# Small matrix products issued in pieces of 32, three steps moved from VectorE to ScalarE, and an earlier split of two head pairs, in a hybrid decoder trunk on one Trainium2 core

## The chip, the cores and the metric

One core of a Trainium2 chip runs the whole kernel. Its engines are TensorE (PE: matrix products; its weight loads are listed as PEld), VectorE (DVE), ScalarE (ACT), GpSimd (POOL) and SyncE (SP), which here issues DMAs. The metric is the device time of one execution in microseconds (us); less is better.

## The reference

One mixer layer over 16 meta tokens and 512 tokens, model width 2048, float32. One input projection feeds three causal mixers that work on different heads; their outputs are gated, joined, projected back and added to the input, and a last RMSNorm follows.

```python
proj = (rms_norm(x, norm_w) @ w_in)                 # 2048 -> about 7600 columns
# A) gated DeltaNet, 6 heads x 128, chunks, triangular solve, state carried from chunk to chunk
# B) GLA, 5 heads (dk 64, dv 128), chunks of 64:
log_g = log_sigmoid(gl @ w_gk2 + b_gk) / 16.0       # gate, bias added before it
g = cumsum(log_g)                                   # within a chunk
attn = einsum('bhid,bhjd,bhijd->bhij', q, k, exp(g_i - g_j))   # causal
k_dec = k * exp(g_last - g);  s = s * exp(g_last) + k_dec^T v
# C) forgetting attention, 5 heads x 128, blocks of 128 queries:
probs = softmax(q @ k^T + c_i - c_j)                # causal, c = cumsum(log f)
o = concat(norm(A) * silu(z), norm(B) * silu(z), C * silu(z))
return rms_norm(x + o @ w_out)[:, 16:]
```

## The kernel before

All large products are made in two float32r halves: an operand `w` is split into `hi` (a rounded copy, made by ScalarE) and `lo` (the rest, made by VectorE), and a product is three matmuls, `hi*hi`, `hi*lo`, `lo*hi`, each of 128x512 (or 128x264 in the pairs below). The stages follow one another on PE like this:

- `pz`, `pg`, `pbdz`, `pbgz`: first gate columns and small gates.
- `px`: the pairs of input columns (DeltaNet's q, k, v; GLA's and attention's k and v), each pair by a scheme of seven half-size products.
- fill blocks `pbgq`, `pbfq`, `pbgz`, `pbfz`: the remaining input columns (queries and gate paths of GLA and attention), 16 groups of three 128x512 matmuls each. They depend on nothing but their operands, so they are what PE does while the mixers wait.
- DeltaNet (`pm`, `pn`, `pym`, `pks`, `p`, `po`), in the order of time between about 512 and 580 us.
- GLA (`gla_load`, `gla_pair`, `gla_levels`, `gla_out`) and attention (`fox_load`, `fox_head`, `fox_block`, `fox_out`), from about 580 to 823 us, side by side.
- the output projection: `po` (three of eight pairs of heads, kp 0 to 2, plus kp 5), `ps` (`SEV`: the four pairs kp 3, 4, 6, 7, again by seven products), and `pz` (the last column block).

**GLA's levels.** `gla_levels` makes the causal 128x128 gate-weighted scores of a pair of heads from small products: for a block size of 64 and 32 together 24 products, then for (16, 8), (4, 2) and (1, 0) 64 products of 32x32 each (half as many for the last, single head). They go to the banks `pss`, one bank for each head. `kx` and `qx` are the scaled keys and queries of a level, `gd` their decay, `at` and `a32` the score tiles. A float32 product that is not a transpose stands as two matmul records and two weight loads in the profile. In `gla_pair`, `gkd` is the block decay times keys, `pkd` the bank of its transposes and of the state products, `gst` the states; `pgo` is the output bank, `gon` its normalised copy. In `gla_load`, `pgk` is the bank of the gate product, `gu` its biased copy.

**Attention's blocks.** `fox_block` makes the logits of 128 queries (`pfa`, `pfd`), takes the maximum (VectorE, `fsm`), the exponential and its sum (ScalarE, `fp`), the reciprocal of the sum (VectorE), multiplies by it, transposes the result on PE into `pfa` and splits it (`ph` by ScalarE, `pl` by VectorE). `fox_out` transposes the meta tokens' part into the bank `pfw`, splits it in four turns between ScalarE (`mh`) and VectorE (`ml`), and then makes the products with the values (`pfw`). `pvf` and `pvgv` are the banks in which attention's and GLA's values (`fv`, `vgv`) are transposed.

**What sets the order.** The program is recorded by a planner, `Weave`: each step is a generator that yields instructions, slots to wait for or events. `Weave.run` always emits the list of instructions with the least planned start plus a priority, and each engine then executes in exactly the order of emission (`pin`). A list that a generator yields is emitted whole. PE's instructions are of two kinds, light (`op.light`: fewer than 64 columns, or fewer than 128 rows or columns of the weights) and heavy; the planner stays in one kind for a turn:

```python
ran = t - self.since
if self.mode:
    other = ran + (sum(o.dur for o in c[3]) if c[3][0].light else 0.0) > LIGHT
else:
    other = ran >= HEAVY
```

A DMA is planned no earlier than the planned end of all DMA traffic less `BACK[...]` (the first number up to a planned time of `BT` on PE, the second after it). Nearly all DMAs are issued by SP in the order of emission; an issue that waits holds back the ones behind it.

**Head pairs.** `finish` hands the gated output of a head over. For the pairs in `STK = (3, 4, 6, 7)`, `seven_heads(kp)` splits both heads and their sums (`oh`/`ol`, `os`, `sh`/`sl`) and sets `e_head`. It starts after `e_d`, which waits for all heads of GLA and attention, or, for a pair in `EARLY_KP`, after GLA and head 10. `seven_operands` splits the weights of `ps` (`wh`, `wl`) once the pairs are there. All instructions carry the line of the planner's call (L283).

Of the kernel before, what the change touches and what calls it, by code (L numbers as in the profile page):

```python
# [8 lines left out]
F32 = mybir.dt.float32  # L9
# [4 lines left out]
AF = mybir.ActivationFunctionType  # L14
ALU = mybir.AluOpType
# [3 lines left out]
P = 128  # L19
D = 2048  # L20
KT = D // P
NM = 16
S = 512
T = NM + S
HT = T // 2
NB = S // P
EPS = 1e-6
H = 3
NN = NB * H
# [52 lines left out]
STP, IP = 0.0, 0.05  # L82
GP, KX = (), 5
AP, KA, XP, GAP = -0.2, 2, 0.3, 0.1
BACK, BT = (3.0, 1.5), 100.0
LIGHT, SLACK, DMAL, STL = 2.0, 0.25, 1.1, 2.5
HEAVY, NEAR = 1.5, 0.05
KW = 2
NXP, SQP, NSL = -0.6, 0.0, 1.5
LP, LSL = 0.1, 1.0  # L90
WP, AOP, HDP = 1.0, -0.6, 0.0
EARLY_KP = ()
STK, KOS, OS0, OSN, OSP = (3, 4, 6, 7), 3, 1, 2, 0.1


# [265 lines left out]
def tile_hybrid_trunk(ctx, tc, xT, xtok, mtok, w_gate, w_first, w_in, w_out, consts, lmask, fin_w, out):  # L361
# [169 lines left out]
    zs, spill = {}, {}  # L531
# [1 line left out]
    e_sp, e_bank = {}, {}  # L533
    sp_of = lambda key: e_sp.setdefault(key, Ev())

    def silu_row(z, key, dst):
        if key[0] == "dz" or key in EARLY:
            yield A.activation(z, z, AF.Silu)
            yield SP.dma_start(out=dst, in_=z)
            return  # L540
        t = yield Get(row_s, f"st{key[0]}{key[1]}")
        yield V.tensor_scalar_max(t[:, :S], z, LOW)
        yield A.activation(t[:, :S], t[:, :S], AF.Exp, scale=-1.0)
        yield A.activation(t[:, :S], t[:, :S], AF.Ln, bias=1.0)
        yield A.activation(t[:, :S], t[:, :S], AF.Exp, scale=-1.0)
        yield VT(out=z, in0=z, in1=t[:, :S], op=ALU.mult)
        row_s.give(t)
        yield SP.dma_start(out=dst, in_=z)
# [174 lines left out]
    def token_rows(key, c, u):  # L723
# [29 lines left out]
    other_pairs = [(("gk", 0), ("gk", 1)), (("gv", 0), ("gv", 1)), (("gv", 2), ("gv", 3)), (("gv", 4), ("gk", 2))] \  # L753
        + [(("fk", h), ("fv", h)) for h in range(FOX_HEADS)]
    PAIRS = [p for c in zip(conv_pairs, other_pairs) for p in c]
    xpart = lambda k0, s: tuple((lambda j, t=t: t[k0 + j][:, s]) for t in (xh, xl))
    tpart = lambda d, s: tuple((lambda j, w=w: d[j // 2][w][:, j % 2, s]) for w in range(2))
    RHS = {1: xpart(0, L), 2: xpart(8, L), 3: xpart(8, R), 4: tpart(tb_, L), 5: tpart(ta, L), 6: tpart(tb_, R),
# [79 lines left out]
    def store(p, n, u):  # L838
        yield VT(out=u, in0=u, in1=rstd, op=ALU.mult)
        key = p.keys[n]  # L840
        if key[0] in CONV:
            c = yield Get(row_s, f"cv{p.i}{n}")
            yield from conv(u, key, c, u)
            if key[0] != "dv":
                yield spilled(key, c)
            W.go(token_rows(key, c, u), -0.1, f"rows{key[0]}{key[1]}", 3.0)
        else:
            yield spilled(key, u)
            sp_of(key).set()
# [252 lines left out]
    def levels(g):  # L1102
        s = gs[g]
        an, xc, xm, um = s.an, s.xc, s.xm, s.um
        uc = yield Get(m_s, f"uc{g}", (P, NN, 32))
        yield V.transpose(uc.rearrange("p n c -> p (n c)"), xc.rearrange("p n c -> p (n c)"))
        pm = yield Get(bank_s, f"pm{g}")
        p3 = pm[:, : NN * 32].rearrange("p (n c) -> p n c", c=32)
        lh = [(slice(64 * q, 64 * q + 32), slice(64 * q + 32, 64 * q + 64)) for q in range(2)]
        yield [PE.matmul(p3[lo_, n, :], an[hi_, n, lo_], uc[hi_, n, :], start=True, stop=True)  # L1110
               for n in range(NN) for lo_, hi_ in lh]
        m1 = yield Get(m_s, f"m1{g}", (P, NN, 32))
        for q in range(2):
            yield A.copy(m1[64 * q : 64 * q + 32], p3[64 * q : 64 * q + 32])
        W.go(state0(g), 0.0, f"state{g}")
        yield V.transpose(um.rearrange("p h c -> p (h c)"), xm.rearrange("p h c -> p (h c)"))
        e_um[g].set()
        yield [PE.matmul(p3[a, n, :], l[lo_, n, :], r[lo_, n, :], start=True, stop=True)
               for n in range(NN) for lo_, hi_ in lh for a, l, r in ((lo_, xc, m1), (hi_, m1, xc))]
        l1 = yield Get(m_s, f"l1{g}", (P, NN, 32))  # L1120
        yield A.copy(l1, p3)
        bank_s.give(pm)
        m_s.give(m1)
        s.uf = uf = yield Get(big_s, f"uf{g}", (P, NN, P))
        yield G.memset(uf, 0.0)
        for r in range(4):
            c = slice(32 * r, 32 * r + 32)
            yield A.copy(uf[c, :, c], uc[c])
        m_s.give(uc)
        for q in range(2):  # L1130
            yield V.tensor_copy(uf[64 * q : 64 * q + 32, :, 64 * q + 32 : 64 * q + 64], l1[64 * q : 64 * q + 32])
# [167 lines left out]
    SC = 1.0 / 16.0  # L1299
# [26 lines left out]
    def gla_load(p, ev):  # L1326
        ne = 2 if p < 2 else 1
        kT, qT, gc = yield from many(Get(w_s, f"g{n}{p}", keep=4) for n in ("kT", "qT", "gc"))
        if p < 2:
            yield from fetch(("gk", p), kT)  # L1330
            yield sp_of(("gq", p))
            yield SP.dma_start(out=qT[:, NM:], in_=spill["gq", p])
        else:
            for t in (kT, qT):
                yield G.memset(t[64:], 0.0)
            yield from fetch(("gk", p), kT[:64], slice(0, 64))
            yield from fetch(("gk", p), qT[:64], slice(64, P))
            yield V.tensor_scalar_mul(qT[:64], qT[:64], 0.125)
        vt = yield from many(Get(w_s, f"vt{p}{e}", keep=4) for e in range(ne))
        vm = yield Get(t_s, f"vm{p}")  # L1340
        yield G.memset(vm, 0.0)
        ev2 = evs(*range(ne))
        for e in range(ne):
            W.go(tok_values(("gv", 2 * p + e), vt[e], vm, e, ev2[e]), GPRI + 0.1, f"gv{p}{e}")
        u = (yield Get(w_s, f"gu{p}", keep=1))
        t = (yield Get(w_s, f"gt{p}", keep=1))
        pg = yield from many(Get(bank_s, f"pgk{p}{a}", keep=1) for a in range(2))
        yield [PE.matmul(pg[a][:, :HT], wgk[:, P * p : P * p + P], misc[:, a * HT : (a + 1) * HT], start=True, stop=True)
               for a in range(2)]
        for a in range(2):  # L1350
            yield V.tensor_scalar_add(u[:, a * HT : (a + 1) * HT], pg[a][:, :HT], bgk[:, p : p + 1])
            bank_s.give(pg[a])
        yield V.scalar_tensor_tensor(out=t, in0=u, scalar=-1.0, in1=u, op0=ALU.mult, op1=ALU.min)
        yield A.activation(t, t, AF.Exp)
        yield A.activation(t, t, AF.Ln, bias=1.0)
        yield V.scalar_tensor_tensor(out=u, in0=u, scalar=0.0, in1=t, op0=ALU.min, op1=ALU.subtract)
        yield V.tensor_tensor_scan(gc, gsc, u, 0.0, ALU.mult, ALU.add)
        w_s.give(u)
        w_s.give(t)
        yield tuple(ev2.values())  # L1360
        ev.set((ne, kT, qT, gc, vt, vm))
# [3 lines left out]
    def gla_levels(p, group, sets, pair, at, a32, ev):  # L1365
# [8 lines left out]
        for s in group:  # L1374
# [10 lines left out]
                        mm.append(PE.matmul(pss[e][o0 : o0 + n, off + b * n : off + b * n + n], kx[rr, k0 : k0 + n],  # L1385
                                            qx[rr, q0 : q0 + n], start=True, stop=True))
            off += NB * n
        yield mm
        for s in group:
            if ops[s][0]:  # L1390
                sets.append(ops[s][0])
# [48 lines left out]
    def gla_pair(p, pair, sets, at):  # L1440
# [6 lines left out]
            W.go(gla_levels(p, g, sets, pair, at, a32, el[g]), GPRI, f"levs{p}{g[0]}")  # L1447
        dd = yield Get(w_s, f"gkd{p}")
        d4 = dd[:, :S].rearrange("p (b t) -> p b t", b=NB)
        yield VT(out=d4, in0=g4[:, :, P - 1 : P].to_broadcast([P, NB, P]), in1=g4, op=ALU.subtract)  # L1450
        yield A.activation(dd[:, :S], dd[:, :S], AF.Exp, scale=SC)
        yield VT(out=d4, in0=d4, in1=k4, op=ALU.mult)
        pk = yield Get(bank_s, f"pkd{p}")
        yield [PE.transpose(pk[:, b * P : (b + 1) * P], dd[:, b * P : (b + 1) * P], ident) for b in range(NB)]
# [83 lines left out]
    ST = STK  # L1538
# [82 lines left out]
    def fox_block(h, b, ld, phi, plo, mt, ev):  # L1621
# [22 lines left out]
        yield A.activation(pr[:, : m + P], pr[:, : m + P], AF.Exp, bias=sm[:, 2:3], accum_out=sm[:, 3:4])  # L1644
        yield V.reciprocal(sm[:, 0:1], sm[:, 3:4])
        yield V.tensor_scalar_mul(m4[:, b, :NM], pr[:, :NM], sm[:, 0:1])
        yield V.tensor_scalar_mul(pr[:, NM : m + P], pr[:, NM : m + P], sm[:, 0:1])
        yield [PE.transpose(pa[:, jb * P : (jb + 1) * P], pr[:, NM + jb * P : NM + (jb + 1) * P], ident)
               for jb in range(b + 1)]
        n = min(b + 1, 3)  # L1650
# [163 lines left out]
                    s.src[kp, n].set(t)  # L1814

    def seven_operands():
        yield tuple(e_head[2 * kp] for kp in ST)
        for s in SEV:
            for n in ORDER:
                for kp in ST:  # L1820
                    src = yield s.src[kp, n]
                    hi = yield Get(d_s, f"wh{s.cp}{kp}{n}", (P, S), F32R)
                    lo = yield Get(d_s, f"wl{s.cp}{kp}{n}", (P, S), F32R)
                    yield A.copy(hi, src)
                    yield VT(out=lo, in0=src, in1=hi.bitcast(F32), op=ALU.subtract)
                    give(src, r_s, d_s)
                    s.op[n, kp].set((hi, lo))
# [271 lines left out]
```

## Time and profile before

| what | value |
|---|---|
| runs shown (device time) | 970.83, 973.27, 974.09 us; median 973.27 |
| the profiled execution: its own time, its span | 971.76 us, 970.0 us |
| granted TensorE clock over the span | 0.995 |
| busy: PE, PEld, DVE, ACT, POOL | 947.7, 844.5, 750.5, 569.6, 67.1 us |
| DMA | 167.18 MB, mean 172 GB/s |
| chain that ended last, by engine | PE 90%, DVE 3%, ACT 3%, issue 1%, DMA 1% |

The span runs from the first to the last instruction; 1.8 us of the execution's own time lie around it. A busy time is the union of an engine's instructions; PE's matmuls overlap in the pipeline, so that a busy PE can still be losing time, and what counts is how far apart they start (0.23 us for 128x512, 0.12 us for 128x264). "Idle before" is the time in which an engine ran nothing before an instruction, and the name behind the arrow is what ended it; "issue" means that no wait in the profile explains it.

### The profile page before, as it was taken

Reading aid. Unit: us, or ns where it says so; the run is one execution under the profiler, and the core shown is the slowest. Engines: PE = TensorE matmul, PEld = TensorE weight load, DVE = VectorE, ACT = ScalarE, POOL = GpSimd, SP = SyncE. Lnnn points to the kernel's source line nnn. Section 1 sums busy time; section 2 is a strip of 40 time slices with the busy share of each in tenths; the row PEclk is TensorE's granted clock in tenths of the full one; section 3 lists DMA queues with packets and bytes.
Section 4 is the critical chain, followed back from the end, with each engine's and each line's share of the span. In section 5 each row is a group of like instructions: output and inputs, shape, how many; then the busy total and the mean of one; then the engine's idle time right before and its main releaser. Section 6 shows DMA issues by size and latency. Waiting matters only on the chain.

```text
span 970.0 us, 19077 instructions
## 1 busy us (share of the span) xinstructions
PE 947.7 (98%) x7283; PEld 844.5 (87%) x7283; DVE 750.5 (77%) x1337; ACT 569.6 (59%) x1205; POOL 67.1 (7%) x118
## 2 busy tenths in 40 slices
PE   9999999999999999999999999989989999999996
PEld 7888999999999999999987997778777787888885
DVE  7986887888888888798973666876866966888775
ACT  7865566667766576654424684637546565345445
POOL 0000101010100101110001111010010100000000
PEclk9999999999999999999999999999999999999999
DMA  9933648658784768692288335423233365474424
GB/s 344 372 113 132 164 136 226 191 150 228 193 228 117 220 154 253 171 229 83 89 290 292 97 88 182 141 85 137 99 100 135 107 207 182 154 261 153 151 67 173
DMA packets 92143, 167.18 MB, mean 172 GB/s; under 512 B 16253, under 2 KB 36477, under 8 KB 92052
## 3 DMA queue, kind: packets, MB, share of 16 engines
q1 hardware_dynamic: 87156, 157.31, 49.2%
q0 software_dynamic: 4608, 8.39, 6.5%
q8 instruction: 57, 0.93, 0.4%
q14 instruction: 34, 0.28, 0.1%
q10 hardware_dynamic: 288, 0.27, 0.1%
HBM read 142.33 MB, written 40.39 MB: 188 GB/s over the span
## 4 chain that ended last, share of the span: by engine, by line
PE 90%; DVE 3%; ACT 3%; issue 1%; DMA 1%; POOL 0%; SPq 0%; DVEq 0%; ACTq 0%; POOLq 0%
PE px L283 38%; PE po L283 9%; PE ps L283 8%; PE pz L283 5%; PE pbfq L283 5%; PE pbfz L283 5%; PE pbgz L283 4%; PE pbdz L283 2%; PE pbgq L283 2%; PE pg L283 1%; PE pss L283 1%; PE pfa L283 1%; PE pks L283 1%; PE pfw L283 1%; PE pgo L283 1%
## 5 line engine op out<-in xcount | busy, mean ns | idle before, releaser
L283 DVE SCALAR_TENSOR_TENSOR lp<-a,hp 128x1024 fp32r<-128x1024 f32 x90 | 110.7, 1231 | 36.9 <-ACT hp L283 36.1
L283 ACT CAST hp<-a 128x1024 fp32r<-128x1024 f32 x90 | 94.5, 1050 | 73.3 <-PE px L283 48.0
L283 PE MATMUL px<-xh,hp 128*128 128x264 f32 x432 | 123.7, 286 | 0.0
L283 PE MATMUL px<-xh,lp 128*128 128x264 f32 x432 | 122.7, 284 | 0.0
L283 PE MATMUL px<-xl,hp 128*128 128x264 f32 x432 | 122.7, 284 | 0.0
L283 PE MATMUL px<-tah,hp 128*128 128x264 f32 x288 | 83.8, 291 | 0.0
L283 PE MATMUL px<-tbh,hp 128*128 128x264 f32 x288 | 82.5, 287 | 0.0
L283 PE MATMUL px<-tbh,lp 128*128 128x264 f32 x288 | 82.3, 286 | 0.0
L283 PE MATMUL px<-tbl,hp 128*128 128x264 f32 x288 | 82.0, 285 | 0.0
L283 PE MATMUL px<-tah,lp 128*128 128x264 f32 x288 | 82.0, 285 | 0.0
L283 PE MATMUL px<-tal,hp 128*128 128x264 f32 x288 | 81.8, 284 | 0.0
L283 PEld LDWEIGHTS px<-xh,hp 128*128 128x128 f32 x432 | 81.4, 188 | 0.1
L283 PEld LDWEIGHTS px<-xh,lp 128*128 128x128 f32 x432 | 81.3, 188 | 0.0
L283 PEld LDWEIGHTS px<-xl,hp 128*128 128x128 f32 x432 | 81.2, 188 | 0.0
L283 PEld LDWEIGHTS px<-tbh,hp 128*128 128x128 f32 x288 | 54.3, 189 | 0.1
L283 PEld LDWEIGHTS px<-tah,hp 128*128 128x128 f32 x288 | 54.2, 188 | 0.1
L283 ACT CAST hp<-s 128x1024 fp32r<-128x1024 f32 x36 | 37.8, 1051 | 28.0 <-PE px L283 19.2
L283 PEld LDWEIGHTS px<-tal,hp 128*128 128x128 f32 x288 | 54.3, 188 | 0.0
L283 PEld LDWEIGHTS px<-tbl,hp 128*128 128x128 f32 x288 | 54.2, 188 | 0.0
L283 PEld LDWEIGHTS px<-tah,lp 128*128 128x128 f32 x288 | 54.2, 188 | 0.0
L283 PEld LDWEIGHTS px<-tbh,lp 128*128 128x128 f32 x288 | 54.2, 188 | 0.0
L283 DVE SCALAR_TENSOR_TENSOR lp<-s,hp 128x1024 fp32r<-128x1024 f32 x36 | 44.0, 1221 | 7.9 <-ACT hp L283 7.9
(406 smaller groups left out, 2642.2 us busy)
## 6 DMA issues: line engine op xcount, KB each, us to landing
a<-in_w_in SPq DMA_DIRECT2D x72, 512.0 KB, 5.7
osum<-in_w_out SPq DMA_DIRECT2D x32, 256.0 KB, 5.0
o<-in_w_out SPq DMA_DIRECT2D x16, 512.0 KB, 3.5
kd<-osum SPq DMA_DIRECT2D x25, 256.0 KB, 3.8
kd<-in_w_out SPq DMA_DIRECT2D x21, 256.0 KB, 4.2
rgz<-in_w_in SPq DMA_DIRECT2D x10, 512.0 KB
rfq<-in_w_in SPq DMA_DIRECT2D x10, 512.0 KB, 3.2
rfz<-in_w_in SPq DMA_DIRECT2D x10, 512.0 KB, 3.2
```

The lines of the kernel that those rows point to most:

```text
L283: self.pin(op.call(*op.a, **op.kw))
```

## The change

```diff
-BACK, BT = (3.0, 1.5), 100.0
-LIGHT, SLACK, DMAL, STL = 2.0, 0.25, 1.1, 2.5
+BACK, BT = (3.0, 3.0), 100.0
+LIGHT, SLACK, DMAL, STL = 1.5, 0.25, 1.1, 2.5
+NOP, CH, CD = 0, 32, 32
-EARLY_KP = ()
+EARLY_KP = (3, 4)
 # levels (DeltaNet), at two places
-        yield [PE.matmul(...) for n in range(NN) for lo_, hi_ in lh]
+        mm = [PE.matmul(...) for n in range(NN) for lo_, hi_ in lh]
+        for i in range(0, len(mm), CD):
+            yield mm[i : i + CD]
 # gla_load
-            yield V.tensor_scalar_add(u[:, a * HT : (a + 1) * HT], pg[a][:, :HT], bgk[:, p : p + 1])
+            yield A.activation(u[:, a * HT : (a + 1) * HT], pg[a][:, :HT], AF.Identity, bias=bgk[:, p : p + 1])
 # gla_levels
-        yield mm
+        for i in range(0, len(mm), CH):
+            yield mm[i : i + CH]
 # gla_pair
-        yield VT(out=d4, in0=g4[:, :, P - 1 : P].to_broadcast([P, NB, P]), in1=g4, op=ALU.subtract)
-        yield A.activation(dd[:, :S], dd[:, :S], AF.Exp, scale=SC)
+        gl = one((P, NB), f"ggl{p}")
+        yield A.activation(gl, g4[:, :, P - 1], AF.Copy, scale=SC)
+        for b in range(NB):
+            yield A.activation(d4[:, b], g4[:, b], AF.Exp, scale=-SC, bias=gl[:, b : b + 1])
 # fox_block
-        yield V.tensor_scalar_mul(pr[:, NM : m + P], pr[:, NM : m + P], sm[:, 0:1])
+        yield A.activation(pr[:, NM : m + P], pr[:, NM : m + P], AF.Copy, scale=sm[:, 0:1])
 # seven_operands
-        yield tuple(e_head[2 * kp] for kp in ST)
+        yield e_d
         for s in SEV:
             for n in ORDER:
+                if n == ORDER[NOP]:
+                    yield tuple(e_head[2 * kp] for kp in ST)
...
```

The lists of small products are yielded 32 at a time, and a light turn of the planner is at most 1.5 of its microseconds long (2.0 before). The scaling of the probabilities by the reciprocal sum, the addition of GLA's gate bias and the block decay are ScalarE's; the decay is four exponentials of 128x128 with a bias in place of one subtraction and one exponential of 128x512. After a planned time of 100 us DMAs may be planned 3.0 instead of 1.5 us ahead of the end of the traffic. The pairs 3 and 4 may be split after GLA. The rest of the diff (a gate path in `store`, `EXTRA`) is reached by no pair of columns. The numbers of instructions on DVE and ACT go from 1339 to 1310 and from 1064 to 1102; those on PE, POOL and SP stay.

Since each list now competes separately, the whole order behind the first pieces differs. Three places:

PE, GLA's first pair of heads. Before, the end of the list for the levels 4 and 2 (`pss_7521`, `pss_7522`), attention's first logits, and the start of the next list (levels 1 and 0):

```order
L283 MATMUL pss_7521<-qx_6892,kx_6877 32x32
L283 MATMUL pss_7522<-qx_6892,kx_6877 32x32
L283 MATMUL pfa_7538<-fk_7012,fq_7014 128x144
L283 MATMUL pfa_7539<-fk_7012,fq_7014 128x272
L283 MATMUL pfa_7540<-fk_7012,fq_7014 128x400
L283 MATMUL pss_7630<-qx_6892,gkT_6917 32x32
L283 MATMUL pss_7631<-qx_6892,gkT_6917 32x32
```

Now, within the list for the levels 4 and 2 (`pss_7559`, `pss_7560`), the end of its first piece and the start of its second:

```order
L285 MATMUL pss_7559<-qx_6901,kx_6894 32x32
L285 MATMUL pss_7560<-qx_6901,kx_6894 32x32
L285 MATMUL pbfz_7532<-xh_255,hbfz_0_7309 128x512
L285 MATMUL pbfz_7532<-xl_256,hbfz_0_7309 128x512
L285 MATMUL pbfz_7532<-xh_255,lbfz_0_7310 128x512
L285 MATMUL pfa_7454<-ident,fp_7461 128x128
L285 MATMUL pbfz_7532<-xh_269,hbfz_0_7309 128x512
L285 MATMUL pbfz_7532<-xl_270,hbfz_0_7309 128x512
L285 MATMUL pbfz_7532<-xh_269,lbfz_0_7310 128x512
L285 MATMUL pss_7559<-qx_6882,kx_6874 32x32
L285 MATMUL pss_7560<-qx_6882,kx_6874 32x32
```

What was one run of 64 products is two, with fill products and a transpose of attention between them.

SP, the start of GLA and attention behind DeltaNet: loads of attention's first keys (`fk`), queries (`fq`), values (`fv`) and gates (`fcb`), a store of queries (`spfq`), and a load of fill weights (`rgz`). Before:

```order
L283 DMA rgz_6814<-in_w_in 128x1024
L283 DMA fk_6878<-spfk_3549 128x528
L283 DMA spfq_6890<-qfq_6887 128x512
L283 DMA fq_6879<-spfq_5878 128x512
L283 DMA rgz_6900<-in_w_in 128x1024
L283 DMA fv_6880<-spfv_3736 128x528
L283 DMA fcb_6930<-gd 128x528
```

Now:

```order
L285 DMA fk_6875<-spfk_3549 128x528
L285 DMA fq_6876<-spfq_5881 128x512
L285 DMA fv_6877<-spfv_3736 128x528
L285 DMA fcb_6898<-gd 128x528
L285 DMA spfq_6896<-qfq_6890 128x512
L285 DMA gkT_6917<-spgk_1472 128x528
L285 DMA rgz_6910<-in_w_in 128x1024
```

A store of queries (`spfq`) stood ahead of the loads of `fq`, `fv` and `fcb`, and a load of fill weights ahead of `fv`; now both stand behind all four loads.

DVE before, at the last block of attention's first head (`fp_7047`: its probabilities):

```order
L283 RECIPROCAL fsm_7048<-fsm_7048 128x1
L283 TENSOR_SCALAR fmt_7020<-fp_7047,fsm_7048 128x16
L283 TENSOR_SCALAR fp_7047<-fp_7047,fsm_7048 128x512
L283 TENSOR_TENSOR pl_7018<-pfa_7024,ph_7013 128x128
L283 SCALAR_TENSOR_TENSOR gd_7132<-ggc_6919 128x8x32
```

ACT now, around the scaling of the same block (`fp_7028`):

```order
L285 ACTIVATE fp_7021<-fp_7021,fsm_7022 128x384
L285 ACTIVATE fp_7028,fsm_7029<-fp_7028,fsm_7029 128x528
L285 CAST ph_6996<-pfa_7009 128x128
L285 ACTIVATE fp_7028<-fp_7028,fsm_7029 128x512
L285 CAST ph_6998<-pfa_7009 128x128
L285 CAST hbfq_0_7149<-rfq_6982 128x1024
```

The scaling stood right behind the reciprocal on DVE; now it stands on ACT, behind the exponential, with one cast between the two.

More of the change, by code (lines that the diff above doesn't have):

```diff
@@ L90 @@
 LP, LSL = 0.1, 1.0
+EXTRA = ()
+NOP, CH, CD = 0, 32, 32
 WP, AOP, HDP = 1.0, -0.6, 0.0
-EARLY_KP = ()
+EARLY_KP = (3, 4)
 STK, KOS, OS0, OSN, OSP = (3, 4, 6, 7), 3, 1, 2, 0.1
@@ L534, in tile_hybrid_trunk, with silu_row @@
     sp_of = lambda key: e_sp.setdefault(key, Ev())
-    def silu_row(z, key, dst):
-        if key[0] == "dz" or key in EARLY:
+    def silu_row(z, key, dst, early=False):
+        if early or key[0] == "dz" or key in EARLY:
             yield A.activation(z, z, AF.Silu)
@@ L755, in tile_hybrid_trunk @@
     PAIRS = [p for c in zip(conv_pairs, other_pairs) for p in c]
+    for i, p in EXTRA:
+        PAIRS.insert(i, p)
     xpart = lambda k0, s: tuple((lambda j, t=t: t[k0 + j][:, s]) for t in (xh, xl))
@@ L840, in store @@
         key = p.keys[n]
-        if key[0] in CONV:
+        if key[0] in ("gz", "fz"):
+            spill[key] = drp.tile([P, S], F32, name=f"sp{key[0]}{key[1]}")
+            yield from silu_row(u[:, NM:], key, spill[key], True)
+            sp_of(key).set()
+        elif key[0] in CONV:
             c = yield Get(row_s, f"cv{p.i}{n}")
@@ L1109, in levels @@
         lh = [(slice(64 * q, 64 * q + 32), slice(64 * q + 32, 64 * q + 64)) for q in range(2)]
-        yield [PE.matmul(p3[lo_, n, :], an[hi_, n, lo_], uc[hi_, n, :], start=True, stop=True)
-               for n in range(NN) for lo_, hi_ in lh]
+        mm = [PE.matmul(p3[lo_, n, :], an[hi_, n, lo_], uc[hi_, n, :], start=True, stop=True)
+              for n in range(NN) for lo_, hi_ in lh]
+        for i in range(0, len(mm), CD):
+            yield mm[i : i + CD]
         m1 = yield Get(m_s, f"m1{g}", (P, NN, 32))
@@ L1117, in levels @@
         e_um[g].set()
-        yield [PE.matmul(p3[a, n, :], l[lo_, n, :], r[lo_, n, :], start=True, stop=True)
-               for n in range(NN) for lo_, hi_ in lh for a, l, r in ((lo_, xc, m1), (hi_, m1, xc))]
+        mm = [PE.matmul(p3[a, n, :], l[lo_, n, :], r[lo_, n, :], start=True, stop=True)
+              for n in range(NN) for lo_, hi_ in lh for a, l, r in ((lo_, xc, m1), (hi_, m1, xc))]
+        for i in range(0, len(mm), CD):
+            yield mm[i : i + CD]
         l1 = yield Get(m_s, f"l1{g}", (P, NN, 32))
```

## The prediction

> **What bounds the kernel now.** I read first the page's busy times and its chain, then the busy times by stage, then what PE waited for between 500 and 825 us.
>
> ```profile
> PE 947.7 (98%) x7283; PEld 844.5 (87%) x7283; DVE 750.5 (77%) x1337; ACT 569.6 (59%) x1205; POOL 67.1 (7%) x118
> ...
> q8 instruction: 57, 0.93, 0.4%
> ...
> PE 90%; DVE 3%; ACT 3%; issue 1%; DMA 1%; POOL 0%; SPq 0%; DVEq 0%; ACTq 0%; POOLq 0%
> ```
>
> PE carries the chain from end to end. The change neither adds nor removes a product, so the time can only move by what PE loses: pauses, a lower clock, and turns between small and large products. The stages (us; busy by engine, with the number of instructions; then granted clock, DMA share, GB/s):
>
> ```profile
> 575.00:825.00 250.00, 238.12 (x2182) 191.24 (x2180) 178.58 (x481) 143.38 (x386) 18.01 (x36) 0.99 0.41 137
> 825.00:970.00 145.00, 137.06 (x604) 111.41 (x602) 108.54 (x181) 68.94 (x131) 0.00 (x0) 0.99 0.48 159
> ```
>
> GLA and attention (575 to 825) leave PE idle for 11.9 us and also keep DVE busy for 179 of 250; from 825 on PE idles only in the 8 us behind its last product. So the place is 500 to 825, and there PE waited for (total, times, longest):
>
> ```profile
> PE pss L283 <- issue: 5.1, 3, 2.6
> PE pfw L283 <- DVE ml L283: 2.0, 3, 1.3
> PE pkd L283 <- DVE gst L283: 1.9, 2, 1.1
> PE pvf L283 <- DMA fv<-spfv: 0.7, 1, 0.7
> PE pm L283 <- DVE uc L283: 0.7, 1, 0.7
> PE pvgv L283 <- DMA vgv<-spgv: 0.7, 1, 0.7
> PE pgo L283 <- ACT gon L283: 0.6, 1, 0.6
> ```
>
> With four smaller ones (0.2 to 0.4 each, 1.2 together) these are 12.9 us; 5.1 of them end for no semaphore, inside GLA's small products. That group first.
>
> **The pauses in the small products.** Stretches around two of the three:
>
> ```profile
> 640.00:644.00 4.00, 3.56 (x209) 2.71 (x193) 2.61 (x14) 0.51 (x2) 0.00 (x0) 1.00 0.91 330
> 646.20:650.00 3.80, 3.76 (x44) 2.84 (x45) 2.64 (x14) 1.80 (x7) 0.00 (x0) 0.55 0.01 2
> 713.20:720.72 7.52, 6.01 (x127) 4.75 (x128) 4.08 (x11) 2.88 (x7) 0.00 (x0) 1.00 0.46 143
> 716.00:720.00 4.00, 3.24 (x107) 2.46 (x106) 1.60 (x4) 1.72 (x5) 0.00 (x0) 1.00 0.50 158
> 720.00:725.00 5.00, 4.27 (x45) 3.40 (x45) 1.82 (x6) 2.43 (x6) 0.00 (x0) 0.66 0.01 3
> ```
>
> From the end of the second pause to the end of the third PE began 127 matmuls and 128 loads: 255 instructions. The page's instruction queue brought 57 packets for 2x7283 of them, 255.5 each. So the pauses stand one packet apart: PE had used one packet up before the next was in. They come where a list of 64 products, 256 instructions, runs off in 1.2 us (rows below). Behind two of the pauses the granted clock fell: a loss of 0.45 of 3.8 us and 0.34 of 5, 1.7 each; in the first, 0.6 us were small products, so I count 3.1 together. Pauses and clock: 8.2 us.
>
> The Trainium skill ("Runtime: NRT & Kernel Launch", section "Instruction fetch mechanics") has the same blocks of 256 instructions, but says that their fetch is hidden behind the rate of issue; the trace's 5.1 us speak against "hidden" for these products, and by that rule the pauses would be something else and would stay (rival B).
>
> *What pieces of 32 do.* In the order 540 small products (2160 instructions, eight packets) stood in 12 runs, and now stand in 18, with at least six large products between most of the pieces; no list of 64 is left whole. A packet then lasts two pieces and two fill turns, about 2x0.8+2x1.4 = 4.4 us instead of 1.2 to 3. But the packet of 713.20 lasted 6.0 us of work and still ended in a pause, right behind another late one; so I do not take them all away: one of three pauses stays, with its share of the clock. Gain 2/3 of 8.2 = 5.5 us; bounds 8.2 and, if the packets come later than before, below nothing (rival C).
>
> *What the extra turns cost.* A turn of 128 records and one of 64, between large products:
>
> ```profile
> 702.16 0.40 PE L283 MATMUL pbgz<-xh,lbgz 128*128 128x512 f32 x1
> 702.49 1.29 PE L283 MATMUL pss<-qx,kx 64*32 64x32 f32 x128
> 703.70 0.50 PE L283 MATMUL pbgz<-xh,hbgz 128*128 128x512 f32 x1
> 704.04 0.39 PE L283 MATMUL pbgz<-xl,hbgz 128*128 128x512 f32 x1
> ...
> 767.42 0.39 PE L283 MATMUL pbfz<-xl,hbfz 128*128 128x512 f32 x1
> 767.65 0.40 PE L283 MATMUL pbfz<-xh,lbfz 128*128 128x512 f32 x1
> 767.98 0.46 PE L283 MATMUL pss<-qx,gkT 64*32 64x32 f32 x32
> 768.25 0.48 PE L283 MATMUL pss<-gqT,gkT 64*32 64x32 f32 x32
> 768.66 0.50 PE L283 MATMUL pbfz<-xh,hbfz 128*128 128x512 f32 x1
> ```
>
> From the large product before to the one behind: 1.54 us for the list, 1.01 for half of it, so 0.48 more for two halves, of which 0.23 (767.42 to 767.65) are a large product that has to run anyway; and the product behind a turn takes 0.34 instead of 0.23. One more turn costs 0.25+0.11 = 0.36. There are six more in GLA and one in DeltaNet: 2.5 us, fully on PE. The bounds: 1.7 (0.25 each) and 2.5.
>
> **The three steps moved to ScalarE.**
>
> ```profile
> L283 DVE TENSOR_SCALAR gu<-pgk,cpk 128x264 f32<-128x264 f32 x6 | 2.8, 486 | 0.7 <-PE pgk L283 0.7
> ...
> L283 DVE TENSOR_SCALAR fp<-fp,fsm 128x512 f32<-128x512 f32 x5 | 2.5, 494 | 0.0
> ```
>
> ```profile
> L283 ACT ACTIVATE gkd<-gkd 128x512 f32<-128x512 f32 x3 | 1.9, 632 | 0.0
> ```
>
> DVE loses 20 scalings (494 ns at 512 columns; I estimate 0.38 on average over 128 to 512, 7.7 us), six additions (2.8) and three subtractions (about 2): 12.5 us. ACT gains 38 instructions, by the 632 ns of 512 columns about 0.45 each for the scalings and 0.3 for the pieces of the decay, less three whole exponentials: some 13 us. DVE goes to 166 of 250, ACT to 156 of 250, so neither becomes a bound, and the totals cost nothing on PE. On the path of one block of attention the scaling becomes 0.14 us longer (632 against 494) plus the change of engine; on ACT it waits for DVE's reciprocal with the casts `hbfz`, `hbfq` and GLA's `gon` behind it, and PE's fill waits for those casts. Cover: fill products that stand ready; without it 0.14 to 0.5 us for each of 20 blocks. I take nothing from this and count it in the waits below.
>
> The Trainium skill ("ScalarE: Activation LUTs", "Rules for kernel authors") would leave multiplications and additions on VectorE. Our rows agree on the single instruction, not on the sum: by the rule the change adds about 3 us (20 times 0.14) to chains that the fill covers; by the busy times it is free.
>
> **Loads, order, and PE's other waits (7.8 us).** SP issued this behind DeltaNet:
>
> ```profile
> 579.34 0.38 SPq L283 DMA_DIRECT2D fk<-spfk  x1
> 585.32 0.32 SPq L283 DMA_DIRECT2D spfq<-qfq  x1
> ...
> 587.10 0.42 SPq L283 DMA_DIRECT2D fv<-spfv  x1
> ```
>
> For 6 us a store held back `fq`, `fv` and GLA's loads. Now it stands behind them, so `fv` can leave some 6 us earlier, while its transposes move forward by only 15 large products (3.5 us): the waits for `fv` and `vgv` (1.4) go. In DeltaNet `xc` now stands ahead of the store of GLA's queries and PE has three more fill products (0.7 us) before `pm`: its 0.7 goes, though two more loads stand ahead of it. Of the three waits of `pfw` for `ml`, two get 15 or more large products of cover (9 before) and go (I take 1.6 of the 2.0), one gets 6 and eight small ones instead of 21 and grows by 0.4. One of the two `gst` waits gets the 14 products of `pfw` as cover (1.0 goes), the `gon` wait gets as much (0.6). That is 5.3 less 0.4, about 4.9. But every place has been dealt anew, by planned and not by measured durations; a quarter of the old 7.8 (2.0) may come back elsewhere. Net gain 2.9, bounds 7.8 and a loss of 3 (the waits gone, each replaced by one like it, plus ACT's order).
>
> **BACK and the head pairs.** Deeper planned DMA changes the order of issue only; in the `px` stage PE waits for no load, cost 0, cover the buffers of `a`. The pairs 3 and 4: in the new order GLA's last head is gated behind attention's last, so the split still stands behind both. Its cover, the `po` products of kp 0 to 2, grows from 168 to 189 after the last `pfw`. It costs and brings 0; if the cover were gone, its 16 VectorE steps, at the 0.49 us of 512 columns some 8 us, would show.
>
> **Sum.** -5.5 (pauses and clock) +2.5 (turns) -2.9 (waits) = -5.9 against the span of 970.0: 964.1, and 965.9 as the execution's own time (971.76, 1.8 more). The median of the runs shown, 973.27, lies 1.5 above that execution, so I predict **967.4 us**.
>
> **Rivals.**
> - **B, the pauses stay.** They belong to the small products themselves, so cutting the lists only moves them. For it: one came at a DMA share of 0.91 and one at 0.50, so late transfers alone do not explain them. Against it: the distance of 255 instructions. Price: +2.5-2.9, so 972.9.
> - **C, slower: more packets come late.** Fetches share the DMA engines with data, and the first pause followed 330 GB/s. With `BACK` at 3.0 more data is queued where the small products run; each late packet costs 1.7 us and two times in three 1.5 us of clock, 2.7. There are eight such packets; at five late ones -8.2+13.5+2.5-2.9 = +4.9: 978.2. It ends above the time before from four on.
> - **D, the waits come back in full**, since ACT in order holds back the casts: -5.5+2.5 and 0: 970.3.
>
> **Chances.** Forecast 0.60 (its own range 961 to 972, from the bounds of waits and pauses), B 0.18, C 0.12, D 0.10. A measurement of this kernel tells about 0.3%, 2.9 us, from no change. Faster than 970.4: 0.50 from the forecast, 0.04 from B, 0.05 from D, so 0.59; slower than 976.2: 0.01, 0.03, 0.11, 0.01, so 0.16; the rest, 0.25, the same. The range is 957.5 to 978: below, all pauses and all waits gone (-8.2-7.8+2.5 gives 959.8, and the product behind each of some 15 waits starts the next 0.11 earlier, 1.7 more); above, C.
>
> **What would show it.** Right: no idle "issue" time in `pss`, or one such pause; a granted clock of 1.00 from 600 to 800; 18 runs of `pss`, each next large product 0.34 after its predecessor; no wait of `pvf` and `pvgv` for DMAs; DVE near 738 and ACT near 583 us busy. Wrong: pauses at distances of 255 instructions as before (B, C), or new lines "PE <- ACT fp", "PE <- DVE ml" of over 1 us.

## The result and the profile after

The changed kernel takes 963.19 us (median of 4 runs, 962.97 to 964.02) against 973.68 (median of 4, 970.83 to 981.57): a ratio of 0.9892, with a 95% interval of 0.9861 to 0.9924, so 0.8 to 1.4% faster. I had said 967.4, with a range of 957.5 to 978. The time lies in the range and on the forecast side; the gain is 10.5 us by the medians and 8.6 by the two profiled spans (970.0 and 961.4), where I had forecast 5.9. The experiments show that this sum was nearer than its parts deserved.

First the page after: busy times, and the chain.

```profile
PE 948.3 (99%) x7283; PEld 844.6 (88%) x7283; DVE 738.5 (77%) x1308; ACT 581.2 (60%) x1243; POOL 66.1 (7%) x118
...
PE 94%; DMA 2%; ACT 2%; DVE 1%; issue 0%; DVEq 0%; POOL 0%; SPq 0%; ACTq 0%; POOLq 0%
```

PE does the same 7283 matmuls with 0.6 us more busy time in a shorter span; VectorE lost the 12 us and ScalarE gained the 12 us that were forecast. "Issue", 1% of the chain before, now rounds to 0%. The busy times by stretch (columns as before) of the changed kernel:

```profile
575.00:825.00 250.00, 247.61 (x2251) 200.18 (x2251) 177.59 (x472) 160.63 (x441) 20.29 (x43) 1.00 0.42 140
600.00:800.00 200.00, 197.77 (x1994) 159.06 (x1995) 146.11 (x405) 132.84 (x357) 16.04 (x33) 1.00 0.39 131
```

In the same 250 us PE now idles 2.4 us instead of 11.9 and gets 69 more matmuls done, at a granted clock of 1.00 instead of 0.99. What PE waited for between 500 and 825 us, the whole list:

```profile
PE pkd L285 <- DVE gst L285: 1.0, 1, 1.0
PE pfw L285 <- DVE ml L285: 0.5, 1, 0.5
PE pvf L285 <- ACT fv L285: 0.4, 1, 0.4
PE pks L285 <- ACT y L285: 0.3, 1, 0.3
PE pss L285 <- DVE qx L285: 0.2, 1, 0.2
PE pkd L285 <- ACT gst L285: 0.2, 1, 0.2
PE pm L285 <- DVE uc L285: 0.2, 1, 0.2
PE pvgv L285 <- ACT vt L285: 0.2, 1, 0.2
```

Together 3.0 us instead of 12.9. The line `pss <- issue` (5.1) is gone whole, and so are the two waits for DMAs. A piece of 32 between its neighbours, from the same trace:

```profile
639.72 0.40 PE L285 MATMUL pbfz<-xh,lbfz 128*128 128x512 f32 x1
640.04 0.76 PE L285 MATMUL pss<-qx,kx 64*32 64x32 f32 x64
640.73 0.50 PE L285 MATMUL pbfz<-xh,hbfz 128*128 128x512 f32 x1
641.07 0.40 PE L285 MATMUL pbfz<-xl,hbfz 128*128 128x512 f32 x1
```

From 639.72 to 640.73 are 1.01 us, and the next large product comes 0.34 later: the two numbers from which the turn was priced.

A ledger of PE's time, from the first matmul to the last: I compare each step, from the start of one matmul to the start of the next, with the usual step for the shapes of these two and of the matmul ahead of them (the median over both traces), and put what is over it down to what ended it. Changes from before to after: usual steps +2.3 us (the extra turns; without the shape of the matmul ahead it is +1.3, because the slower product behind a turn then falls into the rest); between 493 and 830 us waits -5.9, pauses -5.7, steps at a lowered clock -3.0 and the rest +1.0; the first 493 us +1.8 (1.2 of it ahead of the first `px`); the output projection +0.2. That is -9.3; the output behind the last matmul takes 0.7 longer, which leaves the 8.6 of the spans.

### The profile page after: what moved, and what is told of

Its sections match the earlier page's. It is cut to its first block, busy times and chain, and to the rows that moved or that the text cites. A ratio compares the mean times of both kernels' runs of the same rounds, so it can differ in the third digit from the quotient of the medians.

```text
span 961.4 us, 19098 instructions
## 1 busy us (share of the span) xinstructions
PE 948.3 (99%) x7283; PEld 844.6 (88%) x7283; DVE 738.5 (77%) x1308; ACT 581.2 (60%) x1243; POOL 66.1 (7%) x118
## 4 chain that ended last, share of the span: by engine, by line
PE 94%; DMA 2%; ACT 2%; DVE 1%; issue 0%; DVEq 0%; POOL 0%; SPq 0%; ACTq 0%; POOLq 0%
PE px L285 38%; PE po L285 10%; PE ps L285 8%; PE pbfz L285 6%; PE pz L285 6%; PE pbfq L285 5%; PE pbgz L285 5%; PE pbdz L285 2%; PE pks L285 2%; PE pfa L285 1%; PE pg L285 1%; PE pfw L285 1%; PE pss L285 1%; PE pbgq L285 1%; PE pgo L285 1%; DMA sc<-ab 1%
```

## The experiments

Two theories at the start. **Packets:** PE pauses where its instructions run into a packet of 256 that is not there yet, and the pieces cure that. **Order:** the pauses and waits went because the planner dealt everything anew, whichever edit made it do so. Spans are of one profiled execution each, which need not be a typical one; ratios are against the kernel before, run beside each group of kernels (its medians there were 973.1 to 974.2 us). The lists of waits show only the rows that the text needs.

| Kernel | median us (runs) | ratio, 95% interval | span us |
|---|---|---|---|
| before, pieces only | 971.42 (10) | 0.9972, 0.9948 to 0.9995 | 972.1 |
| before, `BACK` only | 962.50 (4) | 0.9890, 0.9828 to 0.9952 | 965.5 |
| before, scalings and additions on ScalarE, own order | 971.06 (10) | 0.9990, 0.9958 to 1.0021 | 976.0 |
| before, borders shifted by 128 | 971.88 (10) | 0.9961, 0.9925 to 0.9997 | 972.0 |
| before, borders shifted by 192 | 978.81 (10) | 1.0047, 1.0015 to 1.0078 | 977.2 |
| after, whole lists | 974.23 (10) | 0.9986, 0.9959 to 1.0013 | 973.3 |
| after, whole lists, no early split | 965.70 (4) | 0.9907, 0.9889 to 0.9925 | 963.4 |
| after, `BACK` as before | 969.56 (4) | 0.9951, 0.9933 to 0.9969 | 966.8 |
| after, scalings and additions on VectorE, own order | 966.53 (4) | 0.9918, 0.9899 to 0.9937 | 965.2 |
| after, borders shifted by 160 | 968.72 (10) | 0.9947, 0.9915 to 0.9980 | 967.0 |
| after, small products twice | 987.66 (4) | 1.0135, 1.0115 to 1.0154 | 986.9 |
| after, `BACK` 4.0 | 975.21 (10) | 1.0005, 0.9976 to 1.0033 | 976.5 |

### Are the pauses packet borders?

**Before, shifted by 128 and by 192 instructions.** The order stays; tiny products are put in behind the warm-up, unseen by the planner (32 here, 48 in the second).

```diff
         yield [PE.matmul(pw[:, :P], ones, ones, start=True, stop=True) for _ in range(9)]
+        for _ in range(32):
+            o = PE.matmul(pw[:32, :32], ones[:64, :32], ones[:64, :32], start=True, stop=True)
+            W.pin(o.call(*o.a, **o.kw))
```

> The kernel before in its own order, with 32 tiny products (128 instructions) added to the warm-up at the start, so that every later packet of 256 instructions begins 128 instructions earlier in the same stream. Packet theory: the pauses move to the new packet borders. The packets of the old trace cut there last 6.8 and then 2.75 us around 640 (one pause of 1 to 3 us, near 642.8 instead of 646), but 8.3, 5.7 and 8.1 us around 711 to 728, so the two pauses there go: span 970 - 3 to -6, about 966. Place theory (the pauses belong to these products, their operands or the data moved at that moment): three pauses at the same products, 970 within 1.5.

> As the shift by 128, with 48 tiny products (192 instructions). Packet theory: the old trace cut at the new borders has packets of 1.4 and 2.4 us one behind the other at 640 to 644, and 5.4 and 1.5 at 711 to 721; so pauses of 2 us and more at the new borders in both places, 4 to 9 us together, span 969 to 975, no better than before though only the borders moved. Place theory: three pauses at the same products as before, 970 within 1.5.

PE's waits that ended for no semaphore, shift 128 and then shift 192:

```profile
PE pss L283 <- issue: 1.5, 1, 1.5
...
PE pn L283 <- issue: 0.9, 1, 0.9
```

```profile
PE pss L283 <- issue: 3.5, 2, 2.4
PE pfa L283 <- issue: 2.7, 1, 2.7
```

```profile
649.70:653.50 3.80, 2.81 (x128) 1.95 (x127) 0.68 (x4) 0.00 (x0) 1.13 (x3) 0.65 0.05 16
```

The pauses left their products and went with the borders. Shift 128: one pause in GLA, 128 instructions ahead of the first of before in the stream, none around 711 to 728, and a new one in DeltaNet's `pn`, which I had not counted. Shift 192: three, one of them in a product of 128 columns (`pfa`), and the last fence shows 128 matmuls and 127 loads between the end of the first and the second: one packet. The warm-up products delay the start (the first `px` comes 6.0 and 3.5 us later than before), so behind the first `px` the kernels take 4.0 us less and 3.8 more than the one before. These are the signs that the packet theory gave, but the second time does not count for it: it also holds a wait of `pm` for `uc` of 2.4 us (0.7 before) and a dip of the clock behind it, some 3.4 together.

Count every instruction of PE from the start: matmuls, weight loads and the few that only wait for a semaphore. All 19 pauses that end for no semaphore and make a step of over 1 us, in the 14 traces of this study, then stand at an instruction of number 193 + 256k. The traces also time each packet of the instruction queue. Before the change the three packets concerned landed at 644.76, 711.80 and 719.33 us, and PE went on at 646.24, 713.23 and 720.73. At all 19 pauses PE went on 1.2 to 1.6 us after the packet had landed, and at none of the 795 borders in these traces did it go on less than 1.2 us after it. The late packets took 0.9 to 1.4 us (the median of all is about 1.0); they had set out late, 1.2 to 6.4 us after PE crossed the border before. So the pauses are waits for the next packet of instructions: that is shown.

**After, every small product twice,** order as it is, so that a piece of 32 is a whole packet.

```diff
-        for i in range(0, len(mm), CH):
-            yield mm[i : i + CH]
+        # two = each product, then a copy of it that the planner takes for free
+        for i in range(0, len(two), 2 * CH):
+            yield two[i : i + 2 * CH]
```

> The changed kernel in its own order, with each of GLA's 540 small products issued twice in a row (same operands, same result), so that a piece of 32 uses up a whole packet of 256 instructions. 540 x 4 instructions of work add about 9 us by themselves (0.0085 us a record). Packet theory: pauses at packet borders come back although pieces and large products stand as in the changed kernel, five or more of them, 5 to 20 us together, with dips of the clock: 975 to 995. Rival (a piece between large products cannot starve PE, however many instructions it has): 961.4 + 9 = 970, no pauses.

The waits, and the largest pause, inside a doubled piece:

```profile
PE pss L285 <- issue: 7.8, 8, 2.0
```

```profile
647.10 0.59 PE L285 MATMUL pss<-qx,kx 64*32 64x32 f32 x38
649.71 1.10 PE L285 MATMUL pss<-qx,kx 64*32 64x32 f32 x90 [2.03 <-issue]
650.74 0.44 PE L285 MATMUL pfa<-ident,fp 128*128 128x128 f32 x2
```

Eight pauses, 7.8 us, in an order that had none: what counts is how many instructions run off in a time, not how many products stand in a piece. The span is 986.9 instead of the 970 of the rival. By the ledger the 25.5 us over the changed kernel hold 9.6 for the usual steps of the added products, 9.3 for the steps with pauses and 3.1 for two dips of the clock.

**After, shifted by 160.** The same 40 tiny products, ahead of `pr`.

> The changed kernel in its own order, with 40 tiny products (160 instructions) put in ahead of the first pr product (at 53 us), so that every later packet border falls 160 instructions earlier in the same stream; they cost about 1.0 us. In the trace of the changed kernel the packets cut there last 4.0 and 3.8 us one behind the other around 640, and 3.8 and 5.1 around 716 to 724; so far PE paused where two packets in a row lasted under about 10.6 us together. Packet theory (the pieces stretch the packets, but the changed kernel is free of pauses also because its borders fall well): one or two pauses at borders, 1 to 4 us together, perhaps with dips of the clock: span 963.5 to 969. Rival (pieces of 32 between large products cure the pauses wherever the borders fall): no pause over 0.5 us, 962.4.

No pause, and no wait over 1 us behind 493 us; from the last `px` to the last `pfw` 316.6 us, in the changed kernel 316.1. Of the 5.6 us more of the span 4.7 lie ahead of it: the tiny products themselves, a wait of 0.7 of `pg` for a load at 245 and waits of `pbgq` (0.7); the rest of the 4.7 is in no single wait. My forecast fell: packets of 4.0 and 3.8 us in a row were in time here, though in the kernel before 6.8 and 2.9 were not. So in this order the pieces hold with the borders at a second place too, and my rule "two packets under 10.6 us pause" is no rule. That they cure the pauses in any order is not shown: in the order of "before, pieces only" (below) one stays. Why one packet sets out late and another does not stays open.

### What are the pieces worth?

**After, with whole lists.**

```diff
-NOP, CH, CD = 0, 32, 32
+NOP, CH, CD = 0, 1000, 1000
```

> The changed kernel with its lists of small products left whole (64 to a list again, 12 runs of pss instead of 18); everything else of the change stays. Packet theory (pauses come where PE uses up packets of 256 instructions faster than they are fetched, and the pieces cured them): pauses of 2 to 6 us with no releaser come back in pss, with 1 to 4 us of lower clock; 2.5 us of turns are saved; span 961.4 - 2.5 + 8 = 967 (963 to 971). Order theory (the new order of the other work took the pauses away): no pauses, span 961.4 - 2.5 = 959.

PE's longest waits:

```profile
PE pfa L285 <- ACT fp L285: 5.0, 1, 5.0
PE pfw L285 <- DVE ml L285: 2.0, 2, 1.8
PE pss L285 <- issue: 2.0, 2, 1.6
```

The whole gain is gone, and only 2.0 us of it in pauses, at the lower end of the packet theory's 2 to 6. The longest wait is new. ScalarE there:

```profile
800.55 0.61 ACT L285 CAST oh<-gz 128x512 fp32r<-128x512 f32 x1
805.14 1.29 ACT L285 CAST sh<-os 128x512 fp32r<-128x512 f32 x2 [3.99 <-DVE os L285]
806.59 0.41 ACT L285 ACTIVATE fp<-fp,fsm 128x144 f32<-128x144 f32 x1 [0.15 <-DVE fsm L285]
```

`oh`, `os`, `sh` are the split of a head pair. With whole lists GLA's last head ends at 791 instead of 808, ahead of attention's, `EARLY_KP` opens, and the split stands in front of attention's last block on both engines. In the changed kernel `EARLY_KP` does nothing: with it empty the program comes out the same, instruction for instruction. The next kernel takes it out of the whole lists.

**After, whole lists, no early split.**

```diff
-EARLY_KP = (3, 4)
+EARLY_KP = ()
```

> The changed kernel with whole lists of 64, as in the first experiment, and EARLY_KP empty, so that no head pair is split behind GLA. In the first experiment PE waited 5.0 us for fp of attention's last block and 0.9 behind it, while VectorE and ScalarE split head pairs (os, oh, ol, sl). Theory: that early split stood ahead of the last block; without it the 5.0, the 0.9 and the lower clock behind them go: span 973.3 - 7 = 966 (964 to 968), pauses in pss near 2 us as there. Rival: attention's last block is late for its own chain of ScalarE and VectorE steps: the wait stays, 971 or more.

```profile
PE pfw L285 <- DVE ml L285: 2.0, 2, 1.8
...
PE pss L285 <- issue: 0.5, 1, 0.5
```

965.7 against 974.2: 8.5 us come back with the split (9.9 by the spans), more than the 7 forecast. On PE the two kernels run in the same order up to 797 us, so this is the price of the split alone. And without any pieces this kernel is 8 us faster than the one before, with 0.5 us of pauses. So the pieces, as they stand in the change, are worth the difference to 963.2: 2.5 us by the medians, 1.5 by the ratios (0.9907 and 0.9892). That is not clear of the noise, as the two intervals overlap.

**Before, with the pieces only** (`CH`, `CD` and `LIGHT` as in the change).

> The kernel before with nothing but the pieces of 32 and the shorter planned turns; divisions, bias, decay, stores and loads as before. Packet theory: no pause, or one of the three; span 970.0 - 8.2 + 2.5 = 964 (961 to 968, the other waits being dealt anew). Order theory: pauses as before plus the turns, 972.

PE's waits and a stretch behind the first of them:

```profile
PE pm L284 <- DVE uc L284: 2.4, 1, 2.4
...
PE pss L284 <- issue: 1.4, 1, 1.4
```

```profile
520.80:524.50 3.70, 3.70 (x53) 3.17 (x54) 1.80 (x3) 0.94 (x2) 0.00 (x0) 0.50 0.76 189
```

Two of the three pauses went and one stayed, as in the prediction; but the time moved by 2.7 us, not 6, with runs from 966.8 to 974.0. In the profiled one, the longest of the ten, PE waited 2.4 us for `uc` in DeltaNet, and the clock then stood at 0.50. The order up to there is that of the kernel before, where this wait was 0.7; behind it stands the load of `xc`, which held the chain for 5.2 us here and 4.0 there. With the same order it was 2.4 in the shift by 192 and 2.2 with the scalings on ScalarE. So this wait differs from one execution to the next, and single spans of these kernels carry it.

### What are the other parts worth?

**After, `BACK` as before,** and **before, with the new `BACK` alone.**

```diff
-BACK, BT = (3.0, 3.0), 100.0
+BACK, BT = (3.0, 1.5), 100.0
```

> The changed kernel with BACK at (3.0, 1.5) as before the change; pieces, ScalarE steps and the rest stay. It deals the order anew from the px stage on. Theory of the prediction (BACK changes the order of issue only and is worth nothing): 961.4 within 3 us, no pauses in pss, other waits shuffled. Rival (the deeper planned DMA is what let loads such as fv arrive in time): waits of pvf and pvgv for DMAs of 0.6 or more each come back, and pm's for uc; 964 to 967.

> The kernel before with BACK at (3.0, 3.0) and nothing else. Theory (BACK lets the loads of fk, fq, fv and vgv go ahead of the store that held them, here as in the changed kernel): the waits of pvf and pvgv for DMAs go (1.4 us), xc stands ahead of the store of GLA's queries, the rest is dealt anew: span 970.0 - 1.5 to -6. Rival (the 5 us that BACK was worth in the changed kernel were the luck of that order alone): 970 or more.

The changed kernel with the old `BACK`, waits of PE and then SP's issues:

```profile
PE ps L285 <- ACT wh L285: 1.7, 1, 1.7
PE ps L285 <- DVE wl L285: 1.4, 1, 1.4
...
PE pbfz L285 <- DVE qfq L285: 1.0, 1, 1.0
...
PE pvf L285 <- DMA fv<-spfv: 0.6, 1, 0.6
PE pvgv L285 <- DMA vgv<-spgv: 0.6, 1, 0.6
```

```profile
581.00 0.38 SPq L285 DMA_DIRECT2D fk<-spfk  x1
586.96 0.32 SPq L285 DMA_DIRECT2D spfq<-qfq  x1
...
588.74 0.42 SPq L285 DMA_DIRECT2D fv<-spfv  x1
```

With the old `BACK` the store of `qfq` again stands ahead of `fv`, and both DMA waits are back; in the changed kernel `fk` goes at 575.20, `fv` at 576.16 and the store at 587.57. So `BACK` moved the store, and no other edit; the rival had this right. Two new waits of `ps`, for its split weights, and one for `qfq` make up most of the 5.4 us by which the span is longer; the waits for `fv` and `vgv` are 1.2 of it. And the kernel before with nothing but the new `BACK`:

```profile
PE pss L283 <- issue: 3.6, 4, 2.0
PE pfw L283 <- DVE ml L283: 1.6, 2, 1.3
PE pkd L283 <- DVE gst L283: 1.2, 2, 0.8
PE pvgv L283 <- DMA vgv<-spgv: 0.6, 2, 0.4
```

962.5: this one number has the whole gain of the change, although its profiled execution still pauses for 3.6 us. `fv` is on time and the store stands behind it, as the theory said; `vgv` is not (0.6 of 0.7 is left). The trace explains only part of the gain: it is of the longest of the four runs (967.3; the others 961.5 to 962.7), and beside the 4.5 us that its span is below the one before (`fv`, less of `pss`, `gst` and `ml`, one dip of the clock instead of two) the other 5 were in runs without a trace. Where they come from stays open.

**After, `BACK` 4.0.**

> The changed kernel with BACK at (3.0, 4.0) instead of (3.0, 3.0); it may beat both. If deeper planned loads help by themselves: 961.4 or less, no wait of PE for a DMA. If 3.0 was worth its 5 us by the luck of its order: other waits come in, 962 to 968, as the order is dealt anew from the last 40 us of the px stage on.

```profile
PE pm L285 <- issue: 3.6, 1, 3.6
```

```profile
540.00:546.00 6.00, 6.00 (x38) 4.84 (x38) 0.13 (x1) 1.68 (x3) 0.00 (x0) 0.51 0.00 0
```

975.2, as slow as before the change, and slower than both forecasts. A border fell into DeltaNet's small products, PE stopped 3.6 us, and the clock stood at half for some 10 us. Deeper is not better here; 3.0 gave an order that came out well.

**The ScalarE steps, order kept.** The planner still sees the changed kernel (or the one before); only the engine of the 26 instructions differs.

```diff
-        yield A.activation(pr[:, NM : m + P], pr[:, NM : m + P], AF.Copy, scale=sm[:, 0:1])
+        o = A.activation(pr[:, NM : m + P], pr[:, NM : m + P], AF.Copy, scale=sm[:, 0:1])
+        o.call, o.a, o.kw = nc.vector.tensor_scalar_mul, (pr[:, NM : m + P], pr[:, NM : m + P], sm[:, 0:1]), {}
+        yield o
```

> The changed kernel in exactly its own order on every engine's program, but the 20 scalings of attention and GLA's six additions of the gate bias are issued on VectorE again at the same places (the block decay stays on ScalarE). VectorE gains some 10 us of work, ScalarE loses 12. Theory of the prediction (the move is worth nothing by itself): within 1.5 us of the changed kernel's 961.4. Rival (VectorE's lighter load is what took PE's waits for gst and ml away): those waits come back, 964 to 967.

> The kernel before in exactly its own order, with attention's 20 scalings and GLA's six additions issued on ScalarE at the same places; lists, loads and block decay as before. Theory (in the changed kernel the move brought 3.8 us, by taking VectorE off the chain that pfa waits for): here PE waits 0.4 us for pfa's operands in 500 to 825, so the move can bring little, 969 to 970, all pauses as before. Rival (the move is worth some 3 us in any order): 966 to 967.

After with VectorE, then before with ScalarE:

```profile
PE pfa L285 <- DVE fp L285: 1.6, 3, 0.6
PE pm L285 <- DVE uc L285: 1.0, 1, 1.0
...
PE pfa L285 <- ACT fp L285: 0.7, 1, 0.7
```

```profile
PE pss L283 <- issue: 5.2, 2, 3.1
PE pfa L283 <- ACT fp L283: 2.6, 5, 0.8
```

In the order that was dealt for ScalarE, VectorE costs 3.8 us of span (3.3 by the medians), of which 2.3 are PE's waits for the scaled `fp` (in the 0.7 of the row that names ScalarE, VectorE's scaling of that block ended only 0.02 us earlier); most of the rest is `pm` and `po` in DeltaNet, where nothing was edited. Neither explanation of this run held: the move was worth more than 1.5 us, and the waits for `gst` and `ml` did not come back. In the order that was dealt for VectorE, ScalarE makes PE wait 2.6 us for `fp`, and the time does not move (0.9990; the profiled execution, 976.0, is of the longest of the ten). In both kernels the wait falls to the engine that the order was not made for.

## Why the prediction was right, and where it was not

- **Pauses and clock, forecast -5.5.** -8.7 by the ledger: all three pauses went, not two. Mis-sized by 3.2; the bound of 8.2 was close. The cause of the pauses, late packets, was right; the cure was only half right. Whole lists in the new order lost 0.5 us to pauses, so the new order by itself takes most of them away. The pieces seem to make pauses rarer: in the six traces with pieces (each product issued once) one of the 19 stands in GLA and attention, in the seven with whole lists twelve, nine of them in the four that share the order of before. The Trainium skill ("Runtime: NRT & Kernel Launch", section "Instruction fetch mechanics") holds that fetch is hidden; the eight pauses of the doubled products (7.8 us) say not at this rate.
- **Extra turns, +2.5.** Usual steps +2.3, within the bounds of 1.7 and 2.5. Right.
- **PE's other waits, -2.9.** -5.9 by the ledger, -4.8 by the lists of waits (7.8 to 3.0), where I had counted 4.9 before the allowance. The named gains were about right: the waits for the loads of `fv` and `vgv` and for `gon` (2.0) went, with 0.6 for ScalarE's `fv` and `vt` in their place, `pm`'s fell from 0.7 to 0.2, `ml` from 2.0 to 0.5, `gst` from 1.9 to 1.2. The term that failed is the 2.0 that I let come back elsewhere: only about 0.6 of it came.
- **Three steps moved, 0.** Wrong in this order (VectorE in place of ScalarE costs 2.3 us in named waits, up to 3.8), right in the order before. The Trainium skill ("ScalarE: Activation LUTs", "Rules for kernel authors") would leave the scalings and additions on VectorE; the single instruction agrees (512 columns: 494 ns there before, 722 to 727 here), but in the changed order the sum went against the rule. The block decay, the third step, was left in both kernels as it stood and was not tried alone.
- **`BACK`, 0.** The step that failed. I wrote that it "changes the order of issue only", and looked for its cost in the `px` stage. In this program the order of issue is what the waits hang on: the new value alone has a ratio of 0.989 (10.6 us), and without it the change keeps less than half its gain (0.9951 against 0.9892). The loads ahead of the store, which I did count (1.4), came from it.
- **Head pairs, 0.** Right, and for the stated reason: in the changed order they stand behind both. A case near the stated condition came true as well: with whole lists the split stood ahead of attention's last block, and 8.5 us showed where I had put "some 8" for a lost cover.

Of the rivals none came: the pauses were no property of the products (B), no packet came late enough to stop PE (C), and the waits fell (D).

The parts do not add up: alone they bring 2.7 (pieces), 10.6 (`BACK`) and nothing (engines), and together 10.5. The shorter turns (`LIGHT`) were not tried alone either. My terms were each read against the order before; that their sum came near does not show that each is the cause that I gave. The time was in the range partly by luck: the sum put the gain on the pieces and on the waits, and the edit that it put at nothing has all of the gain alone.

## What to carry to other kernels

Where a planner orders the program, each of its numbers deals the order anew: run every part of a change alone and every part taken back, before the gain is put down to the part with the best story, and give an edit that "only changes the order" the widest bound, not zero. An edit's own worth can be had by keeping the order and changing one instruction behind the planner's back. Pauses that end for no semaphore are worth counting in instructions, all of the engine's: here equal remainders modulo 256, and a packet of the instruction queue that had just landed, named the cause. Runs of tiny products cut by large ones had fewer of them here, but one stayed.

## What the hardware showed that was not expected

- All 19 pauses stood at a border of 256 PE instructions, also in `pn`, `pm` and `pfa`, and ended 1.2 to 1.6 us after the packet behind the border had landed; the longest was 3.6 us. The same borders paused for different times in executions with the same order on PE: 2.6, 1.0 and 1.5 us before the change, 2.1, none and 3.1 with the scalings on ScalarE.
- PE's clock fell to half behind stops of 1.5 us and more, whatever made PE stop: after pauses, and also, as the stretch below shows, after the 5.0 us wait for `fp` with whole lists. Such a dip lasted 3.4, 6.8 or 10.2 us; one of 3.4 us adds up to 1.7 us to the stop. The clock did not fall behind each stop: the 2.0 us in the doubled piece at 649.71 left the next 4 us at 1.00, the 2.4 for `uc` did not. Where the limit lies is open.

```profile
809.50:813.00 3.50, 3.50 (x10) 2.72 (x10) 1.88 (x12) 1.54 (x5) 0.00 (x0) 0.50 0.00 0
```
